# Eight-pair output projections of an encoder layer: order of VectorE's sums, product order, descriptor buffer

## The chip, the cores and the metric

The kernel runs on one core of a Trainium2 chip. The metric is the device time of one execution in microseconds; the time given for a kernel is the median of its runs. The engines are TensorE (PE, its weight loads shown apart as PEld), VectorE (DVE), ScalarE (ACT), GpSimd (POOL) and SyncE (SP); each works through its own list of instructions in order and waits on semaphores. Transfers are issued by SP and POOL and carried out by 16 DMA engines.

## The reference

One encoder layer on x of 512 x 1024, in fp32: a half-weighted swiglu block (FFN1), a mixer (convolution and a two-way mLSTM), and a second swiglu block (FFN2), each between two rmsnorms.

```python
def swiglu(x, w_in, w_out):
    gate, up = jnp.split(x @ w_in, 2, axis=-1)
    return (jax.nn.silu(gate) * up) @ w_out
...
h = swiglu(rmsnorm(x, norm_ffn1_pre[l]), w_ffn1_in[l], w_ffn1_out[l])
x = x + FFN_RESIDUAL_SCALE * rmsnorm(h, norm_ffn1_post[l])
h = mixer(rmsnorm(x, norm_mix_pre[l]), w_mix_in[l], ...)
x = x + rmsnorm(h, norm_mix_post[l])
h = swiglu(rmsnorm(x, norm_ffn2_pre[l]), w_ffn2_in[l], w_ffn2_out[l])
x = x + FFN_RESIDUAL_SCALE * rmsnorm(h, norm_ffn2_post[l])
```

w_in is 1024 x 5632 (gate and up, 2816 columns each), w_out is 2816 x 1024.

## The kernel before

**Precision.** Every fp32 operand is split into a high part (ScalarE casts, L319) and a low part (VectorE subtracts, L321); a product is three matmuls: high x high, high x low, low x high. `split` (L317 to L322) does this for weights and for left operands. `pin` keeps an instruction in program order on its engine while `pinned` says so; what isn't pinned is placed by the scheduler of the language.

**Weights.** `stream` lists all weight tiles in order of use. `w_load` loads the next ones into one of four raw buffers, `w_split` splits them, `w_get` hands one out and has others split ahead.

**Input projection.** `ffn()` runs for FFN1 and FFN2. Two column blocks are plain (`PLAIN`), the other 20 blocks j use a 2 x 2 scheme with seven products instead of eight: `product(n, ...)` is 12 matmuls of 128x256 (L458). Results are combined by ScalarE copies (L523, L525, L529) and VectorE adds (L531 into the gate's first half, L533 its second, L536 into the up half by product 7). L534 is the silu, L537 and L512 multiply into `h`. Product 4 of block j (`last`, L507 to L512) runs after products 1 and 5 of block j + 1, in a bank that L536 of block j must have read. Of the last block, it stands behind the loop.

**Output projection.** The 22 row blocks of w_out are worked in eight pairs (`SEVEN`) and six plain rows. For each pair, rows 2n (top) and 2n + 1 (low), the same scheme has seven products; products 1, 5, 6, 7 (kind "a") run first for all eight pairs, products 2, 3, 4 (kind "b") later, with plain rows ("k", `mm_out`, L627) between them. `product_out` is 6 matmuls of 128x512 (L602): two row blocks, three matmuls each. All accumulate in the eight PSUM banks.

- Kind "a" in `w_load`: SP loads a quarter of top and a quarter of low into one raw tile (L146, L147); then a POOL transfer that adds (L148) puts top's second half onto both; SP loads top's first quarter ("own", L159) into a tile of its own.
- `w_out_a` (L217 to L234) makes the four right operands: the sum `t` of own and the raw tile's second half (L225, which needs the adding transfer to have landed), then the splits of own, of the raw tile and of t. The sum isn't pinned.
- Kind "b": a POOL transfer adds a quarter of low onto the kept t (L164).
- `left_a` (L578 to L588) makes the left operands of two pairs from `h` by sums (L561) and splits; `left_b` those for kind "b". `taken` (L606 to L619) reads the results of the a products out of PSUM after the last pair.

The loop calls `w_get(2)` in the last column block, so loads, sum and splits of pairs 0 and 1 are issued with the last two column blocks.

## Time and profile before

| what | value |
|---|---|
| median of 3 runs | 928.8 us (928.57 to 929.14) |
| the profiled execution's own time | 929.96 us |
| its span, first to last instruction | 928.2 us |
| TensorE busy | 898.7 us, 97% of the span |
| VectorE busy | 695.2 us, 75% |
| ScalarE busy | 471.0 us, 51% |
| mean granted TensorE clock | 0.985 |
| output projections, first `product_out` to first plain row, FFN1 | 243.2 to 301.5 us |

A row of a timeline gives start and length in us, engine, line, operation, out<-in by the program's names (without numbers), shape, how many; in brackets the idle time of the engine ahead of it and what ended it. In a row of waits stand the total, the number of waits and the longest. In a window's row stand the busy time of each engine and the number of its instructions, the granted clock (1.00 is full speed), the DMA engines' mean busy share and GB/s.

### The profile page before, as it was taken

To read this page: it belongs to the slowest core of one execution; us is meant where nothing else is said; L and a number is where in the kernel's file an instruction comes from. 1 tells how busy PE (TensorE), PEld (TensorE's weight loads), DVE (VectorE), ACT (ScalarE), POOL (GpSimd) and SP (SyncE) were. 2 spreads that over 40 slices of the span, in tenths; PEclk is the share of its full clock that TensorE was granted. 3 is DMA by queue.
4 is the path that set the end of the run, shared out by engine and by line. 5 is a ranking of instruction groups with operands and counts; after the bars stand their busy time and mean duration, and the time that the engine had idled before them with its cause. 6 is when DMAs were issued, how large, how long until landed. Compare 5 with 4: busy or idle time off the path is not lost. (4 is left out here: it accounts for less than half of the span.)

```text
span 928.2 us, 14985 instructions
## 1 busy us (share of the span) xinstructions
PE 898.7 (97%) x5935; PEld 815.3 (88%) x5935; DVE 695.2 (75%) x1079; ACT 471.0 (51%) x803; POOL 80.8 (9%) x100
## 2 busy tenths in 40 slices
PE   9999999999789999999999999999999999889997
PEld 7999999999768888988888888999999999767885
DVE  5978988885769957574666647888888876769845
ACT  6645554554446644555455435555454453547621
POOL 5000000001221201100011000000000001121000
PEclk9999999999879999999999999999999999899999
DMA  8333443344878370343222603233433435788402
GB/s 241 100 94 112 137 117 112 93 129 98 215 148 218 127 234 14 84 121 91 69 69 71 202 0 88 73 91 105 124 92 111 117 92 135 199 172 218 136 27 91
DMA packets 136080, 110.62 MB, mean 119 GB/s; under 512 B 5045, under 2 KB 115657, under 8 KB 136010
## 3 DMA queue, kind: packets, MB, share of 16 engines
q1 hardware_dynamic: 129354, 97.09, 35.3%
q0 software_dynamic: 6656, 12.58, 8.1%
q8 instruction: 46, 0.75, 0.3%
q14 instruction: 24, 0.20, 0.1%
HBM read 107.56 MB, written 2.10 MB: 118 GB/s over the span
## 5 line engine op out<-in xcount | busy, mean ns | idle before, releaser
L458 PE MATMUL ps<-big,whi 128*128 128x256 f32 x1920 | 269.1, 283 | 11.6 <-DVE t L536 7.0
L319 ACT CAST whi<-raw 128x1024 fp32r<-128x1024 f32 x197 | 202.1, 1051 | 121.4 <-DVE raw L186 47.7
L321 DVE TENSOR_TENSOR wlo<-raw,whi 128x1024 fp32r<-128x1024 f32 x193 | 234.0, 1221 | 34.8 <-ACT whi L319 18.3
L458 PEld LDWEIGHTS ps<-big,whi 128*128 128x128 f32 x1920 | 246.3, 191 | 13.5 <-DVE t L536 8.1
L458 PE MATMUL ps<-big,wlo 128*128 128x256 f32 x960 | 153.0, 282 | 0.0
L458 PEld LDWEIGHTS ps<-big,wlo 128*128 128x128 f32 x960 | 131.1, 190 | 0.0
L602 PE MATMUL ps<-whi,big 128*128 128x512 f32 x384 | 125.2, 403 | 1.7 <-ACT big L319 1.5
L602 PEld LDWEIGHTS ps<-whi,big 128*128 128x128 f32 x384 | 74.1, 194 | 19.7 <-ACT big L319 2.7
L602 PE MATMUL ps<-wlo,big 128*128 128x512 f32 x192 | 76.5, 407 | 8.5 <-DVE wlo L321 8.5
L449 PE MATMUL ps<-big,whi 128*128 128x512 f32 x320 | 78.3, 397 | 0.0
L449 PEld LDWEIGHTS ps<-big,whi 128*128 128x128 f32 x320 | 59.6, 188 | 13.7 <-issue 0.2
L458 PE MATMUL ps<-big,ws 128*128 128x256 f32 x480 | 65.6, 280 | 0.0
L627 PE MATMUL ps<-whi,big 128*128 128x512 f32 x192 | 60.9, 393 | 0.0
L148 POOL DMA_DIRECT2D raw<-in_w_ffn_out_dram x16 | 19.7, 1231 | 472.6 <-DVE wlo L321 207.1
L458 PEld LDWEIGHTS ps<-big,ws 128*128 128x128 f32 x480 | 60.4, 188 | 0.0
L602 PEld LDWEIGHTS ps<-wlo,big 128*128 128x128 f32 x192 | 37.6, 196 | 18.5 <-DVE wlo L321 10.9
L529 ACT COPY t<-ps 128x256 f32<-128x256 f32 x40 | 14.9, 371 | 69.5 <-PE ps L458 69.4
L319 ACT CAST big<-big 128x512 fp32r<-128x512 f32 (+1 forms) x48 | 37.0, 801 | 17.5 <-DVE big L561 14.2
L627 PEld LDWEIGHTS ps<-whi,big 128*128 128x128 f32 x192 | 36.0, 188 | 8.0
L321 DVE TENSOR_TENSOR big<-big,big 128x512 fp32r<-128x512 f32 (+1 forms) x48 | 42.6, 913 | 0.2 <-PE ps L602 0.2
L534 ACT ACTIVATE t<-t 128x512 f32<-128x512 f32 x40 | 25.2, 631 | 31.1 <-DVE t L531 29.0
L449 PE MATMUL ps<-big,wlo 128*128 128x512 f32 x160 | 40.4, 395 | 0.0
(212 smaller groups left out, 1233.2 us busy)
## 6 DMA issues: line engine op xcount, KB each, us to landing
raw<-in_w_ffn_in_dram SPq DMA_DIRECT2D x88, 512.0 KB, 4.4
raw<-in_w_ffn_out_dram SPq DMA_DIRECT2D x28, 512.0 KB, 4.2
raw<-in_w_mix_in_dram SPq DMA_DIRECT2D x24, 512.0 KB, 5.2
raw<-in_w_ffn_out_dram SPq DMA_DIRECT2D x32, 256.0 KB, 5.6
raw<-in_w_ffn_out_dram POOLq DMA_DIRECT2D x16, 512.0 KB, 5.7
raw<-in_w_mix_out_dram SPq DMA_DIRECT2D x8, 512.0 KB, 3.5
big<-in_w_ffn_out_dram SPq DMA_DIRECT2D x12, 256.0 KB, 8.1
big<-in_w_ffn_out_dram POOLq DMA_DIRECT2D x8, 256.0 KB, 8.3
```

The source lines that it names most:

```text
L148: nc.gpsimd.dma_start(sums.rearrange("p (g f) -> p g f", g=2), top[:, 512:1024].rearrange("p (g f) -> p g f", g=1).broadcast_to([P, 2, 512 ...
L319: latest["hi"] = nc.scalar.copy(out=hi, in_=src)
L321: latest["lo"] = eng.tensor_tensor(out=lo, in0=src, in1=f32(hi), op=ALU.subtract)
L449: nc.tensor.matmul(o, ww[:, k, :], xk(xT, xx, k, sl), start=n == 0, stop=n == 3 * KD - 1)
L458: pin(nc.tensor.matmul(o, ww[:, k, :], x[xx][:, k, :], start=first and n == 0, stop=n == 11, skip_group_check=True))
L529: nc.scalar.copy(a_[:, h1], x[:, h0])
L534: nc.scalar.activation(c, c, AF.Silu)
L602: nc.tensor.matmul(acc[tb + t][half], left[n][x][:, blk(t)], right[n][y], start=first and x == y == 0, stop=last_ and x == 1, skip_group_c ...
L627: nc.tensor.matmul(acc[tb][half], hT[hh][:, blk(tb)], w[ww][:, blk(half, 512)], start=fresh and hh == ww == 0, stop=k == NF - 1 and hh == ...
```

## The change

- `w_out_a`: the split of own comes first, then the sum t, now pinned, the split of t, and the split of the raw tile last.
- In the last column block `w_load(2)` issues the loads of pairs 0 and 1 (they stood there before too, by `w_get(2)`), and with `ahead_own` set it splits their own quarters at once. Sums and other splits of these pairs come after the silu and the add into the gate's first half of the last block (`mark`, `issue_after`), that is behind the input projection's last products but product 7 and 4.
- Pair 0's product 1 is written ahead of product 4 of the last column block. The PSUM tiles of the output projection are taken in two steps.
- During the output projection VectorE's pinned instructions keep program order, and `taken` joins them; ScalarE's casts aren't pinned there (`pinned["act"]`). The splits of left operands go through `split_free`, which pins nothing.
- The products of a pair run in the order 1, 6, 7, 5 instead of 1, 5, 6, 7. `taken` subtracts out of PSUM directly for product 5, which saves two copies and two subtractions per FFN.
- `pre_norm` of the last two row blocks at the start of FFN1 takes its squares in two halves; the scrap tile `junk` is half as wide.
- The buffer for descriptors of POOL's transfers (`dynamic_dma_scratch_size`) is 2048 instead of 1024.

Line numbers move: L225 is L232 in the changed kernel, L321 is L327 (L332 for left operands), L458 is L468, L512 is L522, L531 is L545, L533 is L547, L536 is L550, L537 is L551, L561 is L572, L602 is L613.

VectorE at the end of FFN1's input projection, before. `t_384` is the tile with the own quarters of pairs 0 and 1, `raw_2869` and `raw_2886` are the raw tiles of pairs 0 and 1, `raw_2746` and `raw_2748` the weights of the last column block, `ps_2770` to `ps_2772` the results of the block before the last:

```order
L225 TENSOR_TENSOR big_231<-t_384_2873,raw_2869 128x512
L533 TENSOR_TENSOR t_382_2775<-ps_2772,t_380_2773 128x256
L225 TENSOR_TENSOR big_231<-t_384_2873,raw_2886 128x512
L321 TENSOR_TENSOR wlo_2763<-raw_2746,whi_2762 128x1024
L512 TENSOR_TENSOR big_230<-ps_2647,t_366_2652 128x256
L321 TENSOR_TENSOR wlo_2767<-raw_2748,whi_2766 128x1024
L321 TENSOR_TENSOR wlo_2877<-t_384_2873,whi_2876 128x512
L531 TENSOR_TENSOR t_382_2775<-ps_2771,t_380_2773 128x256
L321 TENSOR_TENSOR wlo_2877<-big_231,whi_2876 128x512
L536 TENSOR_TENSOR t_381_2774<-ps_2770,t_381_2774 128x256
L537 TENSOR_TENSOR big_231<-t_381_2774,t_382_2775 128x256
```

Both sums stand ahead of the multiply of `last` and of L531 and L536 of the block before the last. VectorE in the changed kernel, at the end of the last block (`ps_2896` to `ps_2898` are its results, `t_388` holds the own quarters, `raw_2877` and `raw_2887` are pairs 0 and 1):

```order
L545 TENSOR_TENSOR t_399_2901<-ps_2897,t_397_2899 128x256
L547 TENSOR_TENSOR t_399_2901<-ps_2898,t_397_2899 128x256
L232 TENSOR_TENSOR big_2996<-t_388_2881,raw_2877 128x512
L572 TENSOR_TENSOR big_226<-big_226 128x2x256
L550 TENSOR_TENSOR t_398_2900<-ps_2896,t_398_2900 128x256
L332 TENSOR_TENSOR big_3110<-big_227,big_3109 128x2x256
L332 TENSOR_TENSOR big_3110<-t_425_3111,big_3109 128x2x256
L327 TENSOR_TENSOR wlo_2884<-big_2996,whi_2883 128x512
L327 TENSOR_TENSOR wlo_3014<-raw_2877,whi_3013 128x1024
L232 TENSOR_TENSOR big_2996<-t_388_2881,raw_2887 128x512
L551 TENSOR_TENSOR big_231<-t_398_2900,t_399_2901 128x256
L572 TENSOR_TENSOR big_227<-big_227 128x2x256
```

Here the sum of pair 0 (first L232 row) stands behind L545 and L547 of the last block, and that of pair 1 seven rows later. Between them are parts of the left operands.

TensorE around product 4 of the last block, before. `ps_2902` is that block's bank; `ps_3014` and `ps_3015` take product 1, `ps_3016` and `ps_3017` product 5 of the pairs; `raw_3061` of pair 2 gave `whi_3071` and `wlo_3072`:

```order
L458 MATMUL ps_2902<-big_455,whi_2766 128x256 x8
L458 MATMUL ps_2902<-big_455,wlo_2767 128x256 x4
L602 MATMUL ps_3014<-whi_3067,big_3102 128x512
L602 MATMUL ps_3015<-whi_3067,big_3102 128x512
L602 MATMUL ps_3014<-whi_3119,big_3101 128x512
L602 MATMUL ps_3015<-whi_3119,big_3101 128x512
L602 MATMUL ps_3016<-wlo_3072,big_3101 128x512
L602 MATMUL ps_3016<-whi_3071,big_3102 128x512
L602 MATMUL ps_3017<-wlo_3072,big_3101 128x512
L602 MATMUL ps_3017<-whi_3071,big_3102 128x512
```

Product 4 stands among the products of pairs 2 and 3, just ahead of the rows that read the split of pair 2's raw tile. TensorE there in the changed kernel (`ps_2896` is the last block's bank; `ps_3047` and `ps_3048` take product 6, `ps_3049` and `ps_3050` product 7, `ps_3045` product 5; `whi_2883` and `wlo_2884` hold own and sum of pair 0, `whi_3013` and `wlo_3014` its raw tile):

```order
L468 MATMUL ps_2896<-big_463,whi_2774 128x256 x8
L468 MATMUL ps_2896<-big_463,wlo_2775 128x256 x4
L613 MATMUL ps_3047<-wlo_2884,big_2998 128x512
L613 MATMUL ps_3047<-whi_2883,big_2999 128x512
L613 MATMUL ps_3048<-wlo_2884,big_2998 128x512
L613 MATMUL ps_3048<-whi_2883,big_2999 128x512
L613 MATMUL ps_3049<-wlo_3014,big_2998 128x512
L613 MATMUL ps_3049<-whi_3013,big_2999 128x512
L613 MATMUL ps_3050<-wlo_3014,big_2998 128x512
L613 MATMUL ps_3050<-whi_3013,big_2999 128x512
L613 MATMUL ps_3045<-wlo_3014,big_2998 128x512
L613 MATMUL ps_3045<-whi_3013,big_2999 128x512
```

Product 4 now stands among the products of pair 0, which follow it in the order 6, 7, 5.

The diff:

```diff
--- before.py
+++ after.py
@@ -80,7 +80,7 @@
     def ch(v):
         return v.rearrange("p (c t) -> p c t", t=P)
 
-    pinned = {"PE": True, "rest": True}
+    pinned = {"PE": True, "rest": True, "act": True}
     latest, mark = {}, {}
 
     def pin(ins):
@@ -158,6 +158,10 @@
                         own = own2.pop(0)
                     nc.sync.dma_start(own, top[:, 0:512])
                     raws = [own, sums]
+                    if ahead_own:
+                        oh, ol = (wpool.tile([P, 1024], F32R, tag="w", name=nm(v)) for v in ("whi", "wlo"))
+                        split(oh[:, 0:512], ol[:, 0:512], own)
+                        raws += [oh, ol]
                     loaded.append((raws, kk))
                     continue
                 if kk == "b":
@@ -209,12 +213,12 @@
             7: q(uh, ul, c[0], c[0]), 4: q(uh, ul, c[1], c[1]),
         }
 
-    kept, spare = [], []
+    kept, spare, ahead_own = [], [], []
 
     def keep():
         return spare.pop() if spare else t2()
 
-    def w_out_a(r0, r1):
+    def w_out_a(r0, r1, ah=None, al=None):
 
         c = (slice(0, 512), slice(512, 1024))
 
@@ -222,13 +226,14 @@
             return wpool.tile([P, 1024], F32R, tag="w", name=nm(n))
 
         t = keep()
-        nc.vector.tensor_tensor(out=t, in0=r0, in1=r1[:, c[1]], op=ALU.add)
+        if ah is None:
+            ah, al = wt("whi"), wt("wlo")
+            split(ah[:, c[0]], al[:, c[0]], r0)
+        pin(nc.vector.tensor_tensor(out=t, in0=r0, in1=r1[:, c[1]], op=ALU.add))
         kept.append(t)
-        ah, al = wt("whi"), wt("wlo")
-        split(ah[:, c[0]], al[:, c[0]], r0)
+        split(ah[:, c[1]], al[:, c[1]], t)
         bh, bl = wt("whi"), wt("wlo")
         split(bh, bl, r1)
-        split(ah[:, c[1]], al[:, c[1]], t)
         return {1: (ah[:, c[0]], al[:, c[0]]), 6: (ah[:, c[1]], al[:, c[1]]),
                 5: (bh[:, c[0]], bl[:, c[0]]), 7: (bh[:, c[1]], bl[:, c[1]])}
 
@@ -317,9 +322,14 @@
 
     def split(hi, lo, src, eng=nc.vector):
         latest["hi"] = nc.scalar.copy(out=hi, in_=src)
-        pin(latest["hi"])
+        if pinned["act"]:
+            pin(latest["hi"])
         latest["lo"] = eng.tensor_tensor(out=lo, in0=src, in1=f32(hi), op=ALU.subtract)
         pin(latest["lo"])
+
+    def split_free(hi, lo, src):
+        nc.scalar.copy(out=hi, in_=src)
+        nc.vector.tensor_tensor(out=lo, in0=src, in1=f32(hi), op=ALU.subtract)
 
@@ -337,7 +347,7 @@
         latest["pow"] = nc.gpsimd.tensor_tensor(out=r[:, 0:w], in0=acc, in1=nhalf[:, 0:w], op=ALU.pow)
         return r[:, 0:w]
 
-    junk = const.tile([P, D], BF16, name="junk")
+    junk = const.tile([P, 512], BF16, name="junk")
 
     def sumsq(src):
         s = sm([P, 1], tag="ss")
@@ -515,7 +525,11 @@
         for j in range(PLAIN, NF):
             if j == PLAIN + 4 and late:
                 late()
-            w = w_get(1 if j < NF - 1 else 2)
+            w = w_get(1 if j < NF - 1 else 0)
+            if j == NF - 1:
+                ahead_own.append(True)
+                w_load(2)
+                ahead_own.clear()
             x, y, z = ps(), ps(), ps()
             a_, u, c = t2(), t2(), t2()
             product(1, w, x, True)
@@ -530,20 +544,17 @@
             product(3, w, y, False)
             nc.vector.tensor_tensor(out=c[:, h1], in0=y[:, h0], in1=a_[:, h1], op=ALU.add)
             product(2, w, z, True)
-            nc.vector.tensor_tensor(out=c[:, h0], in0=z[:, h0], in1=a_[:, h0], op=ALU.add)
-            nc.scalar.activation(c, c, AF.Silu)
+            mark["dve"] = nc.vector.tensor_tensor(out=c[:, h0], in0=z[:, h0], in1=a_[:, h0], op=ALU.add)
+            mark["act"] = nc.scalar.activation(c, c, AF.Silu)
             product(7, w, x, False)
             nc.vector.tensor_tensor(out=u[:, h1], in0=x[:, h0], in1=u[:, h0], op=ALU.add)
             nc.vector.tensor_tensor(out=h[j // 4][:, j % 4, h1], in0=u[:, h1], in1=c[:, h1], op=ALU.mult)
             pending = (j, w, x, c, u)
-        last(*pending)
-
-
-
-
-
-        got = {at: ps() for at in ((2, 0), (3, 0), (2, 1), (3, 1), (0, 1), (1, 1), (0, 0), (1, 0))}
-        acc = [[got[tb, half] for half in range(2)] for tb in range(NT)]
         bank = {1: (2, 0), 5: (2, 1), 7: (0, 0), 6: (0, 1), 2: (2, 0), 3: (2, 1), 4: (0, 0)}
         later, early = slice(256, 512), slice(0, 256)
         ea, eb, xb = bigt(), bigt(), bigt()
@@ -557,8 +568,8 @@
         def hcol(k):
             return h[k // 4][:, k % 4, 0:512]
 
-        def tt(o, a_, b_, op):
-            nc.vector.tensor_tensor(out=o, in0=a_, in1=b_, op=op)
+        def tt(o, a_, b_, op, order=lambda v: None):
+            order(nc.vector.tensor_tensor(out=o, in0=a_, in1=b_, op=op))
 
         def halves(g):
             if g == 1:
@@ -580,19 +591,19 @@
             hi, lo = halves(g)
             s1 = t4()[:, 0:256 * g].rearrange("p (g f) -> p g f", g=g)
             tt(s1, a_[:, :, early], b_[:, :, early], ALU.subtract)
-            split(hi[:, :, 0:256], lo[:, :, 0:256], a_[:, :, later])
+            split_free(hi[:, :, 0:256], lo[:, :, 0:256], a_[:, :, later])
             tt(a_[:, :, early], a_[:, :, later], a_[:, :, early], ALU.subtract)
             tt(a_[:, :, later], a_[:, :, early], b_[:, :, early], ALU.add)
-            split(hi[:, :, 256:512], lo[:, :, 256:512], s1)
-            split(hi[:, :, 512:1024], lo[:, :, 512:1024], a_)
+            split_free(hi[:, :, 256:512], lo[:, :, 256:512], s1)
+            split_free(hi[:, :, 512:1024], lo[:, :, 512:1024], a_)
             return parts(hi, lo, g, {1: 0, 5: 256, 7: 512, 6: 768})
 
         def left_b(i):
             g, a_, b_ = group(i)
             hi, lo = halves(g)
-            split(hi[:, :, 0:512], lo[:, :, 0:512], b_)
+            split_free(hi[:, :, 0:512], lo[:, :, 0:512], b_)
             tt(a_[:, :, early], b_[:, :, later], a_[:, :, later], ALU.subtract)
-            split(hi[:, :, 512:768], lo[:, :, 512:768], a_[:, :, early])
+            split_free(hi[:, :, 512:768], lo[:, :, 512:768], a_[:, :, early])
             return parts(hi, lo, g, {4: 0, 2: 256, 3: 512})
 
         def product_out(n, left, right, first, last_):
@@ -611,12 +622,11 @@
                 if n == 1:
                     nc.scalar.copy(e12, o)
                 elif n == 5:
-                    nc.scalar.copy(e22, o)
+                    tt(e22, o, e21, ALU.subtract, pin)
                 elif n == 6:
-                    tt(e12, o, e12, ALU.subtract)
+                    tt(e12, o, e12, ALU.subtract, pin)
                 else:
-                    tt(e21, o, e12, ALU.subtract)
-                    tt(e22, e22, e21, ALU.subtract)
+                    tt(e21, o, e12, ALU.subtract, pin)
 
         begun = set()
 
@@ -628,6 +638,18 @@
                     acc[tb][half], hT[hh][:, blk(tb)], w[ww][:, blk(half, 512)],
                     start=fresh and hh == ww == 0, stop=k == NF - 1 and hh == 1, skip_group_check=True)
 
+        pinned["rest"], pinned["act"] = True, False
+        lefts = left_a(0)
+        with tc.issue_after(mark["act"].ins), tc.issue_after(mark["dve"].ins):
+            w_split(2)
+        got = {at: ps() for at in ((2, 0), (3, 0))}
+        acc = [[None] * 2 for _ in range(NT)]
+        for t in (2, 3):
+            acc[t][0] = got[t, 0]
+        product_out(1, lefts[0], ready[0], True, False)
+        last(*pending)
+        for at in ((2, 1), (3, 1), (0, 1), (1, 1), (0, 0), (1, 0)):
+            acc[at[0]][at[1]] = ps()
         hs, plain_n = None, 0
         ks = {}
         for at, (kind, n) in enumerate(OUT):
@@ -646,10 +668,10 @@
                         for half in range(2):
                             mm_out(tb, half, n, *ks[n])
             elif kind == "a":
-                if n % 2 == 0:
+                if n % 2 == 0 and n:
                     lefts = left_a(n)
                 left, right = lefts[n % 2], w_get(1)
-                for m in (1, 5, 6, 7):
+                for m in ((1, 6, 7, 5) if n else (6, 7, 5)):
                     product_out(m, left, right, n == 0, n == SEVEN - 1)
                     if n == SEVEN - 1:
                         taken(m)
@@ -661,6 +683,7 @@
                     product_out(m, left, right, n == 0 and m == 4, False)
 
         ring.clear()
+        pinned["rest"] = False
 
         def whole(tb):
             o = []
@@ -701,7 +724,7 @@
     st1 = {}
 
     def rest1(tb):
-        st1[tb] = pre_norm(tb, g_pre, 1)
+        st1[tb] = pre_norm(tb, g_pre)
 
 
     def rows8(rows, base):
@@ -1201,7 +1224,7 @@
     from concourse import mybir as _mybir
     from concourse.bass_utils import run_bass_kernel_spmd as _run
 
-    nc = _bacc.Bacc("TRN2", target_bir_lowering=False, num_devices=1, dynamic_dma_scratch_size=1024)
+    nc = _bacc.Bacc("TRN2", target_bir_lowering=False, num_devices=1, dynamic_dma_scratch_size=2048)
     arrays, args = {}, {}
     for name in _INS:
         a = _np.ascontiguousarray(inputs[name])
```

## The prediction

> **What bounds the kernel now.** I read the page first, then TensorE's waits in order of time, then the engine that each names, then the granted clock around them.

> ```profile
> span 928.2 us, 14985 instructions
> PE 898.7 (97%) x5935; PEld 815.3 (88%) x5935; DVE 695.2 (75%) x1079; ACT 471.0 (51%) x803; POOL 80.8 (9%) x100
> PEclk9999999999879999999999999999999999899999
> ```

> TensorE is the bound, at 97% of the span, and its clock sags in two places, around 235 to 270 us and around 790 to 830 us: the two output projections. The timeline of TensorE there, the idle time ahead of a row and its releaser in brackets:

> ```profile
> 237.01 2.08 PE L458 MATMUL ps<-big,whi 128*128 128x256 f32 x8 [6.21 <-DVE t L536]
> 256.26 1.21 PE L458 MATMUL ps<-big,whi 128*128 128x256 f32 x8 [0.59 <-DVE t L536]
> 262.14 0.79 PE L602 MATMUL ps<-wlo,big 128*128 128x512 f32 x1 [3.27 <-DVE wlo L321]
> 267.29 0.80 PE L602 MATMUL ps<-wlo,big 128*128 128x512 f32 x1 [0.52 <-DVE wlo L321]
> 272.68 1.76 PE L602 MATMUL ps<-whi,big 128*128 128x512 f32 x7
> 274.28 0.39 PE L602 MATMUL ps<-wlo,big 128*128 128x512 f32 x1
> ...
> 791.95 2.07 PE L458 MATMUL ps<-big,whi 128*128 128x256 f32 x8 [3.58 <-ACT t L523]
> 816.06 0.51 PE L602 MATMUL ps<-whi,big 128*128 128x512 f32 x1 [0.92 <-ACT big L319]
> 820.62 0.50 PE L602 MATMUL ps<-wlo,big 128*128 128x512 f32 x1 [3.11 <-DVE wlo L321]
> 836.76 0.50 PE L602 MATMUL ps<-wlo,big 128*128 128x512 f32 x1 [1.65 <-DVE wlo L321]
> 839.04 0.50 PE L602 MATMUL ps<-whi,big 128*128 128x512 f32 x1 [0.62 <-ACT big L319]
> ```

> The idle times add up to 10.6 us in FFN1 (6.21 + 0.59 + 3.27 + 0.52) and 9.9 us in FFN2 (3.58 + 0.92 + 3.11 + 1.65 + 0.62). What follows them runs slowly; the windows give the granted clock (columns: window and its length, busy time of PE, PEld, DVE, ACT, POOL, then clock, DMA share, GB/s):

> ```profile
> 222.00:225.00 3.00, 3.00 (x28) 3.00 (x28) 0.00 (x0) 2.19 (x3) 0.00 (x0) 1.00 1.01 173
> 235.00:241.00 6.00, 3.99 (x18) 3.99 (x19) 5.90 (x12) 4.19 (x8) 2.15 (x2) 0.50 0.72 194
> 262.00:272.00 10.00, 9.34 (x22) 6.71 (x23) 6.99 (x11) 4.58 (x7) 2.53 (x3) 0.51 0.80 168
> 290.00:305.00 15.00, 14.83 (x66) 11.77 (x65) 15.00 (x20) 15.00 (x22) 0.87 (x1) 1.00 0.74 209
> 792.00:798.00 6.00, 6.00 (x30) 6.00 (x31) 6.00 (x11) 4.75 (x10) 1.96 (x2) 0.55 0.74 214
> 820.00:827.00 7.00, 6.38 (x21) 5.01 (x21) 4.48 (x8) 2.30 (x5) 2.07 (x3) 0.76 0.90 171
> ```

> Busy time times the missing clock: 3.99 x 0.50 = 2.0, 9.34 x 0.49 = 4.6, 6.00 x 0.45 = 2.7, 6.38 x 0.24 = 1.5, together 10.8 us. So the stalls and their aftermath cost 10.6 + 9.9 + 10.8 = 31.3 us of the profiled execution. Why VectorE came late, from its timeline:

> ```profile
> 220.10 0.69 DVE L186 TENSOR_TENSOR raw<-raw 128x512 f32<-128x512 f32 x1
> 225.94 0.69 DVE L225 TENSOR_TENSOR big<-t,raw 128x512 f32<-128x512 f32 x1 [5.16 <-DMA raw<-in_w_ffn_out_dram]
> 231.79 0.69 DVE L225 TENSOR_TENSOR big<-t,raw 128x512 f32<-128x512 f32 x1 [4.82 <-DMA raw<-in_w_ffn_out_dram]
> 232.40 1.22 DVE L321 TENSOR_TENSOR wlo<-raw,whi 128x1024 fp32r<-128x1024 f32 x1
> 233.53 0.42 DVE L512 TENSOR_TENSOR big<-ps,t 128x256 f32<-128x256 f32 x1
> 235.93 0.69 DVE L321 TENSOR_TENSOR wlo<-big,whi 128x512 fp32r<-128x512 f32 x1
> 236.53 0.42 DVE L536 TENSOR_TENSOR t<-ps,t 128x256 f32<-128x256 f32 x1
> 244.54 0.43 DVE L531 TENSOR_TENSOR t<-ps,t 128x256 f32<-128x256 f32 x1
> ...
> 259.92 0.69 DVE L225 TENSOR_TENSOR t<-big,raw 128x512 f32<-128x512 f32 x1 [1.91 <-DMA raw<-in_w_ffn_out_dram]
> 260.86 1.22 DVE L321 TENSOR_TENSOR wlo<-raw,whi 128x1024 fp32r<-128x1024 f32 x1
> 274.94 0.69 DVE L225 TENSOR_TENSOR t<-big,raw 128x512 f32<-128x512 f32 x1 [3.29 <-DMA raw<-in_w_ffn_out_dram]
> 287.37 0.69 DVE L225 TENSOR_TENSOR t<-big,raw 128x512 f32<-128x512 f32 x1 [1.71 <-DMA raw<-in_w_ffn_out_dram]
> ...
> 789.95 0.69 DVE L225 TENSOR_TENSOR big<-t,raw 128x512 f32<-128x512 f32 x1 [5.34 <-DMA raw<-in_w_ffn_out_dram]
> ```

> VectorE executes in order. Each L225 sum waits for an accumulating transfer; the sums of pairs 0 and 1 hold it 5.16 and 4.82 us at a point where the input projection still needs it, and L536, queued behind them, runs at 236.53 and releases TensorE at 237.01. The same at 259.92: the split behind that sum (260.86) is what TensorE gets at 262.14. In FFN2 the sum at 789.95 holds VectorE 5.34 us, and ScalarE after it:

> ```profile
> 791.01 0.63 ACT L534 ACTIVATE t<-t 128x512 f32<-128x512 f32 x1 [6.19 <-DVE t L531]
> 791.54 0.35 ACT L523 COPY t<-ps 128x256 f32<-128x256 f32 x1
> ```

> The activation waits 6.19 us for L531, the copy L523 stands behind it, and L523 releases TensorE at 791.95. VectorE (75% busy) lacks order, not capacity.

> **The change part by part.**

> *Early quarter, late sums (pairs 0 and 1).* The sums now stand behind the add L531 of the last column block. That row is at 244.54 now; without the 6.21 us stall and the 2.0 us of slow clock it would be at about 236. The data of pair 0's sum had landed by 225.94 and of pair 1's by 231.79, the latter after waiting its turn, and issued no earlier than:

> ```profile
> 220.01 1.37 POOL L148 DMA_DIRECT2D raw<-in_w_ffn_out_dram  x1 [196.49 <-DVE raw L186]
> 226.18 1.24 POOL L148 DMA_DIRECT2D raw<-in_w_ffn_out_dram  x1 [4.80 <-issue]
> 233.64 0.33 SPq L146 DMA_DIRECT2D raw<-in_w_ffn_out_dram  x1
> ```

> So the two waits (10 us) vanish with 10 and about 5 us of margin, and nothing that was behind them is late: L512, L531 and L536 run as their products end. In their place TensorE finds the first product of pair 0, whose left part and own-quarter split (0.60 us of VectorE, the spacing 235.93 to 236.53) stand ahead of the sums in VectorE's order. ScalarE's casts of the sums are no longer pinned and follow the last activation, so the copy L523 has no sum ahead of it. I count the first junction of both projections as gone: 6.21 + 0.59 + 2.0 in FFN1, 3.58 + 2.7 in FFN2, 15.1 us.

> *Earlier loads of pairs 2 to 7.* The third pair's first load went out at 233.64, because its buffer is freed by a split that stood behind the blocked sums (232.40). Those splits follow 220.10 at once now, so that load moves up by some 9 us, and each later pair reuses the buffer of the pair four (two for the first ones) ahead of it, some 20 us before its sum. An accumulating transfer lands 5.8 us after its issue (220.01 to 225.94) and fills all 16 DMA engines for about 3 us of these (share 1.01 in 222 to 225). One at a time, eight of them end by 220 + 8 x 5.9 = 267; the eighth sum is wanted at 236 + 7 x 5.5 = 274. So the transfers keep ahead even if the larger descriptor buffer did nothing. In SyncE's queue four own quarters now stand together ahead of the fifth pair's two loads, where two stood before: two issues of 0.33 us (the issue at 233.64), covered by those 20 us.

> *The larger descriptor buffer.* The second accumulating transfer stood 4.80 us on "issue" until the first had landed (226.18 against 225.94). With room for two, it goes at about 222. Gain between nothing and 4 us of landing, off the path after the step above; the loss, if two share the engines, is at most the first one's own 3 us, inside the margin of 10. I take nothing.

> *Product order 1, 6, 7, 5 and the sum's place in a pair.* TensorE needs 24 matmuls a pair at (274.28 - 272.68) / 7 = 0.229 us, 5.5 us. VectorE needs per pair: sum, own split, split of the sum, 0.60 each; the split of the raw 128x1024, 1.13 (232.40 to 233.53); and half of the left part of two pairs, (5 x 0.60 + 1.13) / 2 = 2.1: together 5.0 us. It fits, at 92%; the sum and its split come first, the long split last, as product 5 does. So the second junction goes too: 3.27 + 0.52 + 4.6 in FFN1, 0.92 + 3.11 + 1.65 + 0.62 + 1.5 in FFN2, 16.2 us. With no waits left in VectorE's row, 8 x 0.5 = 4 us of lead is what it gathers. Behind the last pair it has to do six subtractions of `taken` (3.6), the first left part of kind b (0.60 + 0.60 + 1.13) and its splits (1.7), 7.6 us, beside 5.5 us of product time and the 4 us of lead. Window 290 to 305 shows VectorE and ScalarE full there and TensorE only just fed (14.83 of 15). TensorE will arrive there some 15 us sooner, VectorE less so; I leave 1.5 us of short waits in each projection, between 0 and the 3.3 us that the worst such wait here cost (262.14).

> *Fewer copies.* Two ScalarE copies and two VectorE subtractions a projection fall away, in that same full stretch; up to 1.2 us, counted inside the 1.5.

> *Halved squares of two row blocks in FFN1's start, smaller junk tile.* A few tenths of ScalarE's time beside TensorE's column products; nothing, and under 1 us if the cover were gone.

> *The slow clock after a gap.* By the row at 262.14, a gap of 3.27 us was followed by ten us at clock 0.51; by 820.62, one of 3.11 us by seven at 0.76; by 836.76, one of 1.65 us by no TensorE row longer than usual. So I let gaps of about 3 us and more carry the slow clock away with them, and charge the 1.5 us left behind at their length alone. [...]

> Sum: 31.3 removed, 3.0 left behind, so 928.2 - 28.3 = 899.9 for the span; the execution's time lies 1.76 above its span (929.96), 901.7; the median of the runs shown (928.8) is 1.16 below it, 900.5. I say 901.

> **The rivals.**

> *A, both junctions freed* (above): 897 (nothing left behind) to 907 (3.3 us twice, and one clock drop of 3 us kept).

> *B, only the first junction freed.* Sums of pairs 2 to 7 still come before their data, because the sums are pinned and VectorE now waits in a fixed order without work to slip in. For it: sum intervals as long as 274.94 to 287.37, 12.4 us. Against: that interval followed buffers freed late. It gives 928.8 - 15.1 = 913.7; 908 to 917 with parts of the second.

> *E, the slow clock of the second junctions stays.* If not the two gaps of 3.27 and 3.11 us but the beat of short matmul groups there lowers the clock, 4.6 + 1.5 us stay: 900.5 + 6.1 = 906.6. Against: matmuls of the same kind, in the same short groups, run at 0.229 us each from 272.68 on.

> *C, it does not do what it says.* The transfers slip as far as the sums do, as they would if pair 0's landed after 236 instead of 225.94. Then stalls only change their names: 927 to 930. Against it stand the 10 us of margin.

> *D, slower.*

> ```profile
> 301.54 0.40 PE L627 MATMUL ps<-whi,big 128*128 128x512 f32 x1
> ```

> Fixed order, with the accumulating transfers as the pace: two in flight and the plain loads share 16 engines that one accumulation already fills (share 1.01), and each sum comes as slowly as the slowest interval now, 12.4 us. The last sum would come at 225.94 + 7 x 12.43 = 313, and the pairs would end some 8 us later (the sum's split and 5.5 us of products), at 321, where the plain rows begin at 301.5 today: 19 us a projection, 38 us, 967. It decides at an interval of (301.5 - 8 - 225.9) / 7 = 9.7 us; today's mean is 8.8 with buffers freed late, the least 5.85 (225.94 to 231.79).
> [...] No trace here shows two accumulations at once.

> **How the numbers follow.** About 0.2% (1.9 us) is what a measurement of this kernel can tell from no change. A 0.66, B 0.19, E 0.05, C 0.05, D 0.05. Faster by over 0.2%: A, B, E and a hundredth of C, 0.91; within: the rest of C, 0.04; slower: D, 0.05. The time is A's, 901. A's own range is 897 to 907; it holds E; to leave out no more than 2 in 10, the upper end goes into B, past its 913.7, to 915, and the lower to 896, a little below all stalls gone (897.5).

> **What would show it.** Right: the waits view names no L225-like sum waiting over 1 us ahead of the last L531-like add; TensorE without a gap over 1 us between 230 and 280; granted clock 1.00 in every window there; pairs ending near 284 instead of 301; the second accumulating issue within 3 us of the first; FFN2 the same. Wrong: TensorE released by VectorE splits after DMA waits in pairs 2 to 7 (B), the first sums waiting at their new place (C), or sums over 9.7 us apart (D).

## The result and the profile after

| | before | after |
|---|---|---|
| median | 928.97 us (928.57 to 930.03, 4 runs) | 899.71 us (898.23 to 900.71, 4 runs) |
| profiled execution: time, span | 929.96, 928.2 us | 899.46, 897.1 us |
| TensorE busy | 898.7 us (97%) | 886.2 us (99%) |
| VectorE busy | 695.2 us | 696.8 us |
| mean granted clock | 0.985 | 0.999 |

The ratio of the times is 0.9682 (95% interval 0.9665 to 0.9699): faster by 29 us. A second set of runs of the changed kernel gave 900.14 us and 0.9674 (0.9654 to 0.9694). 901 had been forecast, with a range of 896 to 915.

The page of the changed kernel: no slice of TensorE's clock is below 9 tenths any more.

```profile
span 897.1 us, 14998 instructions
PE 886.2 (99%) x5935; PEld 806.9 (90%) x5935; DVE 696.8 (78%) x1081; ACT 469.9 (52%) x803; POOL 77.7 (9%) x100
PEclk9999999999999999999999999999999999999999
```

All rows of TensorE's timeline with an idle time of 0.15 us or more in the two projections, and the first plain row (L637) of FFN1:

```profile
270.81 1.20 PE L613 MATMUL ps<-whi,big 128*128 128x512 f32 x4 [0.16 <-ACT whi L324]
282.73 0.84 PE L637 MATMUL ps<-whi,big 128*128 128x512 f32 x3
286.45 0.96 PE L613 MATMUL ps<-wt,big 128*128 128x512 f32 x3 [0.32 <-DVE big L572]
288.19 0.50 PE L613 MATMUL ps<-whi,big 128*128 128x512 f32 x1 [0.30 <-DVE big L572]
289.99 1.90 PE L637 MATMUL ps<-whi,big 128*128 128x512 f32 x7 [0.37 <-DVE big L327]
829.17 0.97 PE L613 MATMUL ps<-wt,big 128*128 128x512 f32 x3 [1.22 <-DVE big L572]
```

Both junctions are free. What is left adds up to 1.15 us in FFN1 and 1.22 us in FFN2. All of it but the 0.16 us at 270.81 lies behind the last pair, where VectorE has the subtractions of `taken`, the left parts of kind b and the splits for the plain rows to do. The first plain row comes at 282.7 instead of 301.5 us. The windows of the slow clock, in the same columns as before:

```profile
235.00:241.00 6.00, 6.00 (x39) 5.35 (x38) 4.36 (x8) 3.74 (x6) 0.29 (x1) 1.00 0.90 253
262.00:272.00 10.00, 9.84 (x44) 7.83 (x43) 8.57 (x13) 4.26 (x6) 4.87 (x5) 1.00 0.93 211
792.00:798.00 6.00, 6.00 (x28) 4.99 (x27) 5.92 (x10) 3.77 (x6) 2.86 (x3) 1.00 1.02 189
820.00:827.00 7.00, 7.00 (x33) 5.79 (x32) 6.51 (x9) 7.00 (x11) 0.00 (x0) 1.00 0.82 221
```

All four stand at clock 1.00. VectorE, GpSimd and SyncE there:

```profile
218.79 1.37 POOL L148 DMA_DIRECT2D raw<-in_w_ffn_out_dram  x1 [194.86 <-DVE ws L327]
220.32 1.21 POOL L148 DMA_DIRECT2D raw<-in_w_ffn_out_dram  x1 [0.16 <-issue]
223.53 0.33 SPq L146 DMA_DIRECT2D raw<-in_w_ffn_out_dram  x1
226.19 0.42 DVE L550 TENSOR_TENSOR t<-ps,t 128x256 f32<-128x256 f32 x1 [0.21 <-PE ps L468]
234.22 0.42 DVE L545 TENSOR_TENSOR t<-ps,t 128x256 f32<-128x256 f32 x1
235.00 0.68 DVE L232 TENSOR_TENSOR big<-t,raw 128x512 f32<-128x512 f32 x1
241.20 0.68 DVE L232 TENSOR_TENSOR big<-t,raw 128x512 f32<-128x512 f32 x1
269.66 0.69 DVE L232 TENSOR_TENSOR t<-big,raw 128x512 f32<-128x512 f32 x1 [0.99 <-DMA raw<-in_w_ffn_out_dram]
274.79 0.69 DVE L232 TENSOR_TENSOR t<-big,raw 128x512 f32<-128x512 f32 x1 [1.05 <-DMA raw<-in_w_ffn_out_dram]
```

The add for product 7 (L550) runs at 226.19 and not at 236.53. The sums of pairs 0 and 1 start at 235.00 and 241.20 and wait for nothing. The second accumulating transfer goes 1.5 us after the first, where it was 6.2 us, and the third pair's first load at 223.53 instead of 233.64. Only the sums of the last two pairs still wait for data, about 1 us each in FFN1, 1.94 and 0.18 us in FFN2. TensorE feels little of it: the 0.16 us at 270.81 is the only gap in its rows there.

### The profile page after: what moved, and what is told of

Its sections match the earlier page's. It is cut to its first block, busy times and chain, and to the rows that moved or that the text cites. A ratio compares the mean times of both kernels' runs of the same rounds, so it can differ in the third digit from the quotient of the medians.

```text
span 897.1 us, 14998 instructions
## 1 busy us (share of the span) xinstructions
PE 886.2 (99%) x5935; PEld 806.9 (90%) x5935; DVE 696.8 (78%) x1081; ACT 469.9 (52%) x803; POOL 77.7 (9%) x100
## 4 chain that ended last, share of the span: by engine, by line
PE 82%; DVE 8%; DMA 6%; ACT 2%; issue 2%; POOL 0%; DVEq 0%; POOLq 0%; SPq 0%; ACTq 0%
PE ps L468 40%; PE ps L459 12%; PE ps L613 7%; PE ps L637 7%; PE ps L1197 5%; PE ps L491 4%; DVE wlo L327 3%; PE ps L819 3%; DMA raw<-in_w_ffn_out_dram 2%; DMA t<-in_w_ffn_out_dram 2%; DMA raw<-in_w_ffn_in_dram 2%; DVE big L332 1%; DVE big L572 1%; ACT whi L324 1%; PE ps L1112 1%
## 5 line engine op out<-in xcount | busy, mean ns | idle before, releaser
L468 PE MATMUL ps<-big,whi 128*128 128x256 f32 x1920 | 265.0, 280 | 0.7 <-ACT whi L324 0.7
L327 DVE TENSOR_TENSOR wlo<-raw,whi 128x1024 fp32r<-128x1024 f32 x193 | 233.6, 1219 | 35.5 <-ACT whi L324 20.2
L468 PEld LDWEIGHTS ps<-big,whi 128*128 128x128 f32 x1920 | 243.0, 188 | 1.3 <-ACT whi L324 1.1
L468 PE MATMUL ps<-big,wlo 128*128 128x256 f32 x960 | 151.6, 280 | 0.0
L468 PEld LDWEIGHTS ps<-big,wlo 128*128 128x128 f32 x960 | 129.7, 188 | 0.0
L613 PE MATMUL ps<-whi,big 128*128 128x512 f32 x384 | 122.2, 390 | 0.5 <-DVE big L572 0.3
L613 PEld LDWEIGHTS ps<-whi,big 128*128 128x128 f32 x384 | 71.8, 188 | 16.2 <-DVE big L572 0.9
L613 PE MATMUL ps<-wlo,big 128*128 128x512 f32 x192 | 74.8, 389 | 0.0
L459 PEld LDWEIGHTS ps<-big,whi 128*128 128x128 f32 x320 | 59.5, 188 | 13.7 <-issue 0.2
L468 PE MATMUL ps<-big,ws 128*128 128x256 f32 x480 | 65.6, 280 | 0.0
L637 PE MATMUL ps<-whi,big 128*128 128x512 f32 x192 | 60.7, 394 | 0.4 <-DVE big L327 0.4
L468 PEld LDWEIGHTS ps<-big,ws 128*128 128x128 f32 x480 | 60.4, 188 | 0.0
L148 POOL DMA_DIRECT2D raw<-in_w_ffn_out_dram x16 | 19.6, 1222 | 442.6 <-DMA raw<-in_w_ffn_out_dram 212.7
L637 PEld LDWEIGHTS ps<-whi,big 128*128 128x128 f32 x192 | 35.8, 188 | 8.9 <-DVE big L327 1.0
L613 PEld LDWEIGHTS ps<-wlo,big 128*128 128x128 f32 x192 | 36.0, 188 | 7.4
L637 PE MATMUL ps<-wlo,big 128*128 128x512 f32 x96 | 37.1, 393 | 0.0
L331 ACT CAST big<-big 128x512 fp32r<-128x512 f32 (+1 forms) x32 | 26.0, 837 | 20.2 <-DVE big L332 10.4
L459 PEld LDWEIGHTS ps<-big,wlo 128*128 128x128 f32 x160 | 30.0, 188 | 7.0
```

Source lines behind the costliest of these rows:

```text
L148: nc.gpsimd.dma_start(sums.rearrange("p (g f) -> p g f", g=2), top[:, 512:1024].rearrange("p (g f) -> p g f", g=1).broadcast_to([P, 2, 512 ...
L327: latest["lo"] = eng.tensor_tensor(out=lo, in0=src, in1=f32(hi), op=ALU.subtract)
L331: nc.scalar.copy(out=hi, in_=src)
L459: nc.tensor.matmul(o, ww[:, k, :], xk(xT, xx, k, sl), start=n == 0, stop=n == 3 * KD - 1)
L468: pin(nc.tensor.matmul(o, ww[:, k, :], x[xx][:, k, :], start=first and n == 0, stop=n == 11, skip_group_check=True))
L613: nc.tensor.matmul(acc[tb + t][half], left[n][x][:, blk(t)], right[n][y], start=first and x == y == 0, stop=last_ and x == 1, skip_group_c ...
```

## The experiments

The theory was that VectorE's place and order of the sums decide. The rivals: the larger descriptor buffer decides; the product order decides; ScalarE's freedom decides.

| run | kernel | median us | ratio to before (95%) |
|---|---|---|---|
| 1 | after, sums early again | 905.9 | 0.9753 (0.9713 to 0.9793) |
| 2 | after, small buffer | 907.0 | 0.9763 (0.9729 to 0.9798) |
| 3 | after, order not kept | 911.7 | 0.9812 (0.9773 to 0.9852) |
| 4 | before, large buffer | 915.3 | 0.9857 (0.9817 to 0.9896) |
| 5 | after, first transfers 10 us later | 905.7 | 0.9728 (0.9706 to 0.9750) |
| 6 | after, first transfers 15 us later | 913.6 | 0.9831 (0.9811 to 0.9852) |
| 7 | after, old product order | 898.6 | 0.9665 (0.9645 to 0.9686) |
| 8 | after, own quarters not split ahead | 902.0 | 0.9698 (0.9678 to 0.9718) |
| 9 | after, small buffer and old product order | 920.5 | 0.9890 (0.9869 to 0.9910) |
| 10 | after, ScalarE pinned | 899.1 | 0.9672 (0.9647 to 0.9696) |
| 11 | after | 900.1 | 0.9674 (0.9654 to 0.9694) |
| 12 | after, small buffer, kind b transfers last | 901.0 | 0.9686 (0.9658 to 0.9714) |

Runs 2, 5 and 12 have the changed kernel's order of instructions on TensorE, VectorE and ScalarE, and run 9 has run 7's on all engines. Run 4 has the order of the kernel before, but for the squares in halves. In runs 1, 3, 6, 7, 8 and 10 the scheduler also places some unpinned rows elsewhere, so the edit shown is not the only thing that differs.

**1. The place of the sums.**

```diff
                 ahead_own.clear()
+                w_split(2)
...
-        with tc.issue_after(mark["act"].ins), tc.issue_after(mark["dve"].ins):
-            w_split(2)
```

> The changed kernel with one thing undone: the sums and splits of pairs 0 and 1 are issued in the last column block of the input projection again, where the kernel before has them. Theory (order): the sums wait for their accumulating transfers at a place where the input projection still needs VectorE, so TensorE's stall ahead of product 4 of the block before the last comes back. With two transfers in flight pair 1's sum lands some 3 to 4 us sooner than the 231.79 us of before, so the stall is 2 to 4 us per projection instead of 6.2 and 3.6, with little slow clock: 905 to 911 us. The second junction stays free. Rival (buffer): the larger descriptor buffer is what took the waits away, and the place of the sums is free: 899 to 902 us.

Measured: 905.9 us. Its timeline, first TensorE, then VectorE:

```profile
233.25 1.21 PE L468 MATMUL ps<-big,whi 128*128 128x256 f32 x8 [2.47 <-DVE t L551]
778.01 1.21 PE L468 MATMUL ps<-big,whi 128*128 128x256 f32 x8 [1.23 <-ACT t L538]
225.52 0.69 DVE L232 TENSOR_TENSOR big<-t,raw 128x512 f32<-128x512 f32 x1 [4.75 <-DMA raw<-in_w_ffn_out_dram]
228.03 0.69 DVE L232 TENSOR_TENSOR big<-t,raw 128x512 f32<-128x512 f32 x1 [1.49 <-DMA raw<-in_w_ffn_out_dram]
```

The same two releasers as before, at the same two places, with the sums waiting 4.75 and 1.49 us (5.16 and 4.82 before): with two transfers in flight the second sum follows 2.5 us behind the first, not 5.9. The place alone is worth 6 us in this company, as the order theory said; the buffer is not the whole cure.

**2. The descriptor buffer.**

```diff
-dynamic_dma_scratch_size=2048
+dynamic_dma_scratch_size=1024
```

> The changed kernel with the descriptor buffer of 1024 again; orders on all engines are the same. Theory (order): accumulating transfers go one at a time, pair 1's lands at about 230.5 us, still 10 us ahead of its sum at 241.2; later sums have margins of some us: 899 to 902 us. Rival (buffer): VectorE waits for the sums of pairs 1 to 7 in its fixed order, at least 2 us per projection and pair: 905 us or more.

Measured: 907.0 us. The time is the rival's, 7 us more, but nothing waits at the first junction, and not every pair waits: pairs 6 and 7 do in FFN1, pairs 5 to 7 in FFN2. The timeline of the late pairs:

```profile
268.83 1.19 PE L613 MATMUL ps<-whi,big 128*128 128x512 f32 x4 [0.88 <-ACT whi L324]
817.25 2.08 PE L613 MATMUL ps<-whi,big 128*128 128x512 f32 x4 [3.76 <-ACT whi L324]
806.62 0.69 DVE L232 TENSOR_TENSOR t<-big,raw 128x512 f32<-128x512 f32 x1 [2.74 <-DMA raw<-in_w_ffn_out_dram]
816.11 0.69 DVE L232 TENSOR_TENSOR t<-big,raw 128x512 f32<-128x512 f32 x1 [4.29 <-DMA raw<-in_w_ffn_out_dram]
806.90 0.87 POOL L168 DMA_DIRECT2D big<-in_w_ffn_out_dram  x1 [6.08 <-issue]
808.94 1.20 POOL L148 DMA_DIRECT2D raw<-in_w_ffn_out_dram  x1 [1.17 <-issue]
816.43 1.22 POOL L148 DMA_DIRECT2D raw<-in_w_ffn_out_dram  x1 [6.28 <-issue]
```

The sums of pairs 5 and 6 wait, ScalarE's cast waits for the sum, TensorE for the cast. GpSimd's queue shows where the time goes: transfers stand on "issue" for 1.17 to 6.28 us in these rows, and those of kind b (L168) stand between those of kind a (L148). The one at 806.90 (kind b) goes 0.3 us after pair 5's sum has its data (806.62). The one at 816.43 goes 0.3 us after pair 6's sum has that of 808.94 (816.11, 7.2 us after its issue). The one at 808.94 goes 9.0 us after one of kind b (799.91); that it stood waiting for this one is an estimate from these times. In GpSimd's rows of this run one of kind b goes as little as 0.7 us behind one of kind a (784.34 behind 783.61), but no two of kind a go less than 5.9 us apart (797.30 behind 791.38).

**12. The same with kind b last.** The edit keeps all of GpSimd's accumulating transfers in program order, on top of the small buffer:

```diff
-                    nc.gpsimd.dma_start(
+                    tc.keep_in_program_order(nc.gpsimd.dma_start(
                         sums.rearrange("p (g f) -> p g f", g=2), 
...
-                    nc.gpsimd.dma_start(kept[0], aps[0][:, 0:512], accum_op=ALU.add)
+                    tc.keep_in_program_order(nc.gpsimd.dma_start(kept[0], aps[0][:, 0:512], accum_op=ALU.add))
```

> The changed kernel with the descriptor buffer of 1024, and GpSimd's accumulating transfers of kind b kept behind all eight of kind a (in the run with the small buffer four of kind b stand between them). Orders on TensorE, VectorE, ScalarE and SyncE are those of the run with the small buffer. Theory (with one transfer at a time the transfers of kind b in GpSimd's queue made the sums of pairs 5 to 7 late): the eighth transfer of kind a goes out about 3 us sooner, the stalls of 0.9 and 3.8 us there go: 899 to 904 us. Rival (a single accumulating transfer already takes 7 to 8 us beside the plain loads, so the sums are as late without those of kind b): 905 to 908 us.

Measured: 901.0 us. The last two transfers of kind a and their sums in FFN1, and the sum in FFN2 that waited 4.29 us in run 2:

```profile
260.15 1.21 POOL L148 DMA_DIRECT2D raw<-in_w_ffn_out_dram  x1 [5.38 <-DMA raw<-in_w_ffn_out_dram]
267.92 1.22 POOL L148 DMA_DIRECT2D raw<-in_w_ffn_out_dram  x1 [6.55 <-issue]
267.62 0.69 DVE L232 TENSOR_TENSOR t<-big,raw 128x512 f32<-128x512 f32 x1 [0.98 <-DMA raw<-in_w_ffn_out_dram]
273.58 0.69 DVE L232 TENSOR_TENSOR t<-big,raw 128x512 f32<-128x512 f32 x1 [1.89 <-DMA raw<-in_w_ffn_out_dram]
810.65 0.69 DVE L232 TENSOR_TENSOR t<-big,raw 128x512 f32<-128x512 f32 x1 [0.89 <-DMA raw<-in_w_ffn_out_dram]
```

One transfer of kind a at a time is just enough in this run, with nothing between: of the later sums none waits more than 1.89 us in FFN1 and 1.72 us in FFN2. So in the changed kernel the larger buffer pays because kind b gets into kind a's queue (907.0 us in run 2, 901.0 us here). The gain is mostly in FFN2: in FFN1 the eighth transfer goes at 267.92, against 267.99 in run 2. With that queue in order, half the buffer gives a time within 0.2% of the changed kernel's.

**3. The kept order.**

```diff
-        pinned["rest"], pinned["act"] = True, False
```

> The changed kernel without keeping program order during the output projections (sums, splits and subtractions as the scheduler places them, ScalarE's casts not pinned either). In VectorE's order the sums of pairs 2 and 3 then stand right behind those of pairs 0 and 1, ahead of the add for product 7 of the last block and of pair 0's splits. Theory (order): those two sums wait for transfers issued at about 230 us, landing at about 236 and 239, and hold up the add and the splits by 2 to 5 us in each projection; more later: 904 to 914 us. Rival (the place of pairs 0 and 1 alone decides): 899 to 902 us.

Measured: 911.7 us. The sums of pairs 2 and 3 stand right behind those of pairs 0 and 1 there, and later sums also come before their data:

```profile
242.54 0.50 PE L613 MATMUL ps<-wlo,big 128*128 128x512 f32 x1 [1.94 <-DVE wlo L327]
271.28 0.50 PE L613 MATMUL ps<-wlo,big 128*128 128x512 f32 x1 [4.32 <-DVE wlo L327]
792.80 0.50 PE L613 MATMUL ps<-wlo,big 128*128 128x512 f32 x1 [2.03 <-DVE wlo L327]
239.21 0.69 DVE L232 TENSOR_TENSOR big<-big,raw 128x512 f32<-128x512 f32 x1 [2.30 <-DMA big<-in_w_ffn_out_dram]
269.40 0.69 DVE L232 TENSOR_TENSOR t<-big,raw 128x512 f32<-128x512 f32 x1 [3.88 <-DMA raw<-in_w_ffn_out_dram]
```

As expected: the fixed order is worth 12 us. The larger part of it lies in the second junction (4.32 us at 271.28 and another 2.15 us in FFN2, against 1.94 and 2.03 us in the first), where the order keeps each sum behind work that TensorE needs sooner.

**4. The buffer alone.** The kernel before with the larger buffer. Its two companions in the change go with it: half a scrap tile, and with that the squares of the last two row blocks in halves.

```diff
+junk = const.tile([P, 512], BF16, name="junk")
+st1[tb] = pre_norm(tb, g_pre)
+dynamic_dma_scratch_size=2048
```

> The kernel before with the descriptor buffer of 2048, and with what makes room for it (scrap tile of half the width, squares in two halves for two row blocks); no other change. Theory (order): VectorE still waits at the same place, but pair 1's sum lands some 3 to 4 us sooner, so the first stall of each projection shrinks to about 2 us and its slow clock goes; later sums still hold VectorE: 912 to 922 us. Rival (one transfer at a time was not what the sums waited for): 927 to 931 us. Rival (buffer is the whole cure): 905 us or less.

Measured: 915.3 us, 14 us of the 29, with these stalls and windows:

```profile
230.59 1.21 PE L458 MATMUL ps<-big,whi 128*128 128x256 f32 x8 [2.56 <-DVE t L536]
781.45 1.21 PE L458 MATMUL ps<-big,whi 128*128 128x256 f32 x8 [1.49 <-ACT t L523]
254.10 0.80 PE L602 MATMUL ps<-wlo,big 128*128 128x512 f32 x1 [4.31 <-DVE wlo L321]
```

```profile
230.00:234.00 4.00, 3.41 (x29) 3.41 (x30) 3.90 (x8) 4.00 (x9) 2.69 (x3) 1.00 0.67 174
254.00:261.00 7.00, 6.90 (x18) 5.30 (x19) 6.86 (x11) 4.17 (x6) 1.66 (x2) 0.56 0.66 163
```

The first stall shrinks from 6.21 to 2.56 us (FFN2: from 3.58 to 1.49 us) and the clock stays at 1.00 behind it; the second junction stays. No transfer of kind b stands between those of pairs 0 and 1, so at the first junction the buffer pays by letting pair 1's transfer go sooner: both are through GpSimd by 219.5 us in FFN1 (from 216.87, 2.66 us for the two), where in the kernel before the second went 6.2 us after the first. So 14 us could be had without any new order; the parts overlap and don't add up (14 of the buffer alone, 7 as the last part).

**5 and 6. How late the first transfers may be.** GpSimd adds four columns of a silu to the raw tiles of pairs 0 and 1 and subtracts them again (a rounding is all that changes), which ties their accumulating transfers to that silu; the program order of these instructions is kept.

```diff
+for op in (ALU.add, ALU.subtract):
+    tc.keep_in_program_order(nc.gpsimd.tensor_tensor(out=sums[:, 0:4], in0=sums[:, 0:4], in1=after, op=op))
...
+fn(pending[3][:, 256:260])   # run 5: silu of the block before the last
+fn(c[:, 0:4])                # run 6: silu of the last block
```

> The changed kernel with the accumulating transfers of pairs 0 and 1 held back until the silu of the block before the last is done (GpSimd adds four of its columns to the raw tile and subtracts them again, which ties the transfers to it; the values change by a rounding only), and GpSimd's accumulating transfers kept in program order. Orders of TensorE, VectorE and ScalarE are the same. Theory (margin of about 10 us at the new place): issued at about 227.5 instead of 218.8 and 220.3 us, landing at about 233.5 and 236.5, still ahead of the sums at 235.0 and 241.2: 898 to 903 us. Rival (every us by which a sum lands later costs): 8 us later in each of two projections, 905 us or more.

> The same, but the two accumulating transfers are held back until the silu of the last block (235.7 us). Theory (margin): they land at about 242.3 and 245.3 us, 7 and 4 us after the place of their sums; VectorE waits about 7 us at the first sum, behind it the add for product 7 of the last block, so TensorE stalls some 5 us in each projection, with some slow clock: 908 to 917 us, the stall released by VectorE or ScalarE around 243 us. Rival (the new place has nothing behind it that TensorE needs soon): 899 to 904 us.

Run 5 gave 905.7, outside the theory's 898 to 903. The time is the rival's, its mechanism is not: that the first sums' data land later costs next to nothing by itself. Run 5's first transfers were issued at 228.5 and 231.3 us; at the first junction TensorE waits for nothing in FFN1 and 0.24 us in FFN2, and FFN1's other waits are those of the changed kernel to 0.02 us. Most of the loss is one stall in pair 6 of FFN2, with a granted clock of 0.76 in the window behind it (817 to 824):

```profile
817.80 2.05 PE L625 MATMUL ps<-whi,big 128*128 128x512 f32 x4 [3.09 <-ACT whi L332]
816.66 0.69 DVE L240 TENSOR_TENSOR t<-big,raw 128x512 f32<-128x512 f32 x1 [5.03 <-DMA raw<-in_w_ffn_out_dram]
805.85 1.20 POOL L152 DMA_DIRECT2D raw<-in_w_ffn_out_dram  x1 [5.92 <-DMA raw<-in_w_ffn_out_dram]
```

So the margin at the new place is there, and used up: in FFN2 the first sum already waits 0.97 us. The transfers behind it have none to give in FFN2: the seventh needs 10.8 us from issue to sum. For most of that time the DMA engines are full (share 1.10 from 810 to 817); what else delays it was not tried. Run 6 gave 913.6: the transfers go at 234.2 and 236.4 and land past the old place of their sums, and TensorE stalls, released by the cast of the sum. The last two rows are VectorE's:

```profile
243.11 2.93 PE L625 MATMUL ps<-whi,big 128*128 128x512 f32 x6 [5.37 <-ACT whi L332]
794.01 2.93 PE L625 MATMUL ps<-whi,big 128*128 128x512 f32 x6 [7.31 <-ACT whi L332]
235.44 0.42 DVE L562 TENSOR_TENSOR t<-ps,t 128x256 f32<-128x256 f32 x1 [2.24 <-PE ps L476]
240.41 0.69 DVE L240 TENSOR_TENSOR big<-t,raw 128x512 f32<-128x512 f32 x1 [2.20 <-DMA raw<-in_w_ffn_out_dram]
```

This is not the stall that was expected. The scheduler has put the add for product 7 of the last block (L562) ahead of the first sum (L240), so nothing of the input projection is held up; TensorE works off what it has and then lacks the operands of pair 0. Still, the prediction's limit for the data of pair 0, 236 us, lies between the two runs: landing just ahead of the sum at 235.58 they cost nothing in FFN1 (run 5), landing at 240.4 they cost 5.37 us there (run 6). The time of the rival "it does not do what it says", 927 to 930, was not reached.

**7, 9 and 10. Product order and ScalarE.** Run 7 takes the products as 1, 5, 6, 7 in all pairs but the last and splits the raw tile ahead of the sum, as before:

```diff
-for m in ((1, 6, 7, 5) if n else (6, 7, 5)):
+for m in ((1, 6, 7, 5) if n == SEVEN - 1 else (1, 5, 6, 7) if n else (5, 6, 7)):
```

> The changed kernel with the products of a pair in the order 1, 5, 6, 7 again (but in the last pair, whose results are taken in the new order), and the split of the raw tile ahead of the split of the sum as before. Theory (VectorE's place and fixed order decide, the product order only has to fit the order of splits): 898 to 904 us. Rival (product 5 in second place needs the 1.13 us split too early): short stalls of 1 us in each pair, 907 us or more.

898.6 us: with the larger buffer the new product order is worth nothing. Run 9 adds the small buffer to run 7:

> The changed kernel with both the descriptor buffer of 1024 and the old order of products and splits; orders of TensorE, VectorE and ScalarE are those of the run with the old products. Theory: the raw tile is split sooner, so that SyncE starts the plain loads of pairs 4 to 7 some 2 to 3 us sooner (239.0 against 241.35, 253.6 against 256.8 in the runs with the large buffer), and part of what one transfer at a time costs is given back: 900 to 905 us against 907.0 with the small buffer alone. Rival (one at a time on GpSimd's queue sets the pace of the last sums, plain loads don't matter): 905 to 909 us.

920.5 us, far off both expectations. The eighth pair:

```profile
283.41 1.22 PE L613 MATMUL ps<-whi,big 128*128 128x512 f32 x2 [8.88 <-ACT whi L324]
281.67 0.69 DVE L232 TENSOR_TENSOR t<-big,raw 128x512 f32<-128x512 f32 x1 [8.19 <-DMA raw<-in_w_ffn_out_dram]
270.15 0.86 POOL L168 DMA_DIRECT2D big<-in_w_ffn_out_dram  x1 [3.88 <-issue]
273.08 1.22 POOL L148 DMA_DIRECT2D raw<-in_w_ffn_out_dram  x1 [2.07 <-issue]
```

In this kernel two transfers of kind b stand in GpSimd's queue between the seventh and the eighth of kind a, where one stands in FFN1 of run 2 and none in FFN2. The eighth goes at 273.08, and its sum waits 8.19 us (FFN2: a TensorE stall of 6.64 us). In run 7 the same order with the larger buffer costs nothing. Run 12 showed that such neighbours cost; that they are the whole of run 9's loss, and not the order of splits too, was not tried apart. So with the small buffer the two orders are not alike: 907.0 us with the new one, 920.5 us with the old. Run 10 keeps ScalarE's casts in program order:

```diff
-pinned["rest"], pinned["act"] = True, False
+pinned["rest"], pinned["act"] = True, True
```

> The changed kernel with ScalarE's casts of weights kept in program order during the output projections. Theory (VectorE's order decides; ScalarE, half idle, only has to have no waiting sum ahead of a copy): 898 to 904 us. Rival (casts that wait for a sum hold up the casts of raw tiles and left operands behind them): stalls of 1 us and more released by ScalarE in several pairs, 905 us or more.

899.1 us: no difference.

**8. The early split of the own quarters.**

```diff
-                ahead_own.append(True)
```

> The changed kernel without splitting the own quarters of pairs 0 and 1 ahead: all splits of these pairs come behind the last block's silu. Theory (the early split only fills TensorE's time between product 2 and product 7 of the last block): product 1 of pair 0 gets its operand at about 237.5 instead of 229.6 us; product 7 and product 4 of the last block go first where the order lets them, the rest is a stall of 1 to 3 us in each projection: 901 to 906 us. Rival (it hides anyway): 898 to 901 us.

902.0 us, with waits of 0.52 us in each projection at product 4 of the last block, where 1 to 3 us had been expected. The intervals of the ratios of this run and of the changed kernel overlap, so the 2 us are not clear of noise. Run 11 repeats the changed kernel:

> The changed kernel itself, on the chip of the two runs above, to compare them with: 898 to 901 us, and a ratio to the kernel before between 0.966 and 0.971.

900.1 us. Runs 7, 10 and 11 can't be told apart, so no version was found that beats the changed kernel.

## Why the prediction was right, and where it was not

- **First junction** (15.1 us): the stalls and the slow clock are gone (1.00 in the windows 235 to 241 and 792 to 798, against 0.50 and 0.55), and where the sums are put back (run 1) the old releasers return, L551 and L538. The place of the sums is enough here: run 2 has no wait at this junction with the small buffer. It is not the only cure: with the larger buffer alone (run 4) the stalls are down to 2.56 and 1.49 us, at clock 1.00 (windows 230 to 234 and 781 to 785). Run 3 adds that the next sums must not move up to the first ones.
- **Second junction** (16.2 us): gone too, but for a reason that the prediction had only half. "The transfers keep ahead even if the larger descriptor buffer did nothing" failed: run 2 lost 7 us. The step "eight of them end by 220 + 8 x 5.9 = 267" counted only the transfers of kind a at the best interval seen. In run 12, with nothing of kind b between, the eight go in FFN1 at intervals of 6.1 to 9.1 us beside the plain loads, the last at 267.92, and its sum waits until 273.58; in run 2 kind b stands between as well. The buffer's term, taken as nothing, is about 7 us in the changed kernel, and 14 us in the kernel before. That the sum came out right all the same is luck in this step: the change holds the buffer whose worth the prediction put at nothing.
- **Left behind**: 3.0 us forecast, 2.4 us measured (1.15 + 1.22), nearly all at the place that was named, `taken` and the first left parts of kind b.
- **The sum**: the span was forecast as 899.9 and is 897.1. TensorE's busy time fell by 12.5 us, not by the 10.8 us of the four windows; with 0.6 us less left behind, that is 2.3 of the 2.8 us. Where the other 1.7 us of busy time come from is not shown: just behind the four windows the clock before is back at 1.00 (241 to 256, 272 to 300, 798 to 820, 827 to 845).
- **Product order**: the prediction credited it with a part of the second junction, "the long split last, as product 5 does". Run 7 shows that it is worth nothing with the larger buffer; with the small one, runs 2 and 9 differ by 13 us.
- **Fewer copies**: two copies a projection fall away, but no subtraction, other than the change's description and the prediction have it: `taken` does six of them before and after. The instruction counts agree: ScalarE has 807 in run 4 and 803 in the changed kernel, VectorE 1081 in both. This part had no run of its own, nor had the place of pair 0's product 1.
- **Rivals**: B did not come, with the buffer as it is; run 2 is a mild B, with its late sums in pairs 5 to 7. D did not come. Accumulations that overlap, which it feared, cost little in the changed kernel: in FFN1 the first two go 1.5 us apart and land 5.7 and 6.7 us after their issue, long ahead of their sums; the slowest takes 9.9 us, and the last two sums wait 1 us each. Other than the prediction has it, the trace before shows two at once already: one of kind a at 237.81 (7.3 us to landing) and one of kind b at 238.54 (8.4 us). Run 9 is slow in a fixed order paced by transfers, as D has it, but with one of kind a at a time (6.0 to 10.0 us apart), and its 920.5 us are still less than before. E is out: the slow clock of the second junctions went with the gaps (1.00 in the windows 262 to 272 and 820 to 827, against 0.51 and 0.76).

## What to carry to other kernels

Where an engine that works in order holds an instruction that waits for a transfer, ask what stands behind it and who needs that soonest: the same sums, a few rows later, cost nothing (here 5.16 and 4.82 us of waiting in FFN1 before, none after). Before counting on transfers to keep ahead, write down everything that shares their queue, in the order in which it stands there, not only the transfers that the change is about. Parts of such a change overlap: the same buffer was worth 14 us alone, 7 us as the last part, 22 us beside the old product order, and nothing that could be measured once its queue was in order.
